# Low part of a split weight behind its high part in one chunk of a query projection (encoder block in fp32 on Trainium2)

## The chip, the cores and the metric

The kernel runs on one core of one Trainium2 chip. The metric is the device time of one execution in microseconds (us). For the kernel before, three runs gave 1444.93, 1439.76 and 1440.73 us; their median is 1440.73 us.

## The reference, cut to what matters

One encoder layer on a sequence of 1024 tokens of width 1024, with 16 learned meta tokens ahead of them, all in float32. Two attention branches read the same projection: branch A is differential attention (4 heads), branch B is windowed grouped-query attention (8 query heads, 2 key and value heads, a window of 128 tokens, and sinks).

```python
h = jnp.concatenate([meta, x], axis=1)
for layer in range(DEPTH):
    h = h + mixer_block(rms_norm(h, norm_mix[layer]), ...)
    h = h + swiglu(rms_norm(h, norm_ffn[layer]), w_ff_gate[layer], w_ff_up[layer], w_ff_down[layer])
return rms_norm(h, norm_final)[:, N_META:]
...
proj = h @ w_in                  # 1024 x 4352: qa, ka, va, qb, kb, vb, ga, gb
y_a = differential_attention(qa, ka, va, ...)
y_b = windowed_gqa(qb, kb, vb, sink)
merged = jax.nn.sigmoid(ga) * (y_a @ w_ba) + jax.nn.sigmoid(gb) * (y_b @ w_bb)
return merged @ w_o
```

The change concerns the part `qb` of `proj`: the queries of branch B. Their 512 columns are worked on in four blocks of 128; the change touches the second block.

## The kernel before, in words

**Products.** Every float32 product is made of three faster products of type fp32r. An operand is split into a high part (a copy that is rounded to fp32r, made by ScalarE, L117) and a low part (the operand less its high part, made by VectorE or GpSimd, L118), and high x high, high x low and low x high are added up in one PSUM bank. A weight column block of 1024 x 128 is loaded by `prep` (L174 to L188): one DMA of 512 KB on SyncE's queue (L180), the high part, then the low part. The low part is GpSimd's work, but for a list of blocks (`on_vector`) and the second query block it is VectorE's.

**A projection** (`project_steps`, L207 to L218) goes over chunks of tokens. One chunk has a PSUM bank (tag "pp", three of them) and 8 steps, one for each 128 rows of the weight (`DC` is 8); a step issues three products (L214): wh with hT_hi, wh with hT_lo, wl with hT_hi. hT_hi and hT_lo are the two parts of the normalised input, transposed. Behind the last step the chunk is evicted (`evac_split`, L227): ScalarE writes the high part, VectorE the low part of a staging tile (qk_stage, three of them), and small DMAs on SyncE's queue move it on: 8 for a chunk of keys (L282, with 8 more at L285 for the last chunk), 4 for a chunk of queries of branch B (L305).

**The start of the program** (L411 to L465) interleaves two things. The normalisation and transposition of nine token tiles (`norm_x`, `turn_x`) make the input, 128 tokens at a time, and three projections use it as it comes in chunks of 256 tokens (`early`): p_kb (keys of branch B), p_q0 and p_q1 (first and second query block). The weights of p_q1 are prepared at L434 under the name qbx; both parts of them stand in one tile, wb_qbx, and the low part is VectorE's work, which also works for the normalisation. So the first chunk of p_q1 (tile pp_qb_0) comes about when its weight has just arrived.

**What follows.** The attention of branch B works in units of 128 tokens (`attend_b`): scores (bps, L331), exps on ScalarE (bs, L337, and a small one, bes, L339), scaling by GpSimd (L343), then, in the unit's second half, transposes (bpt, L356) and value products (bpy, L362). Units 0 and 1 are begun at L502; the others (`units_b`, L655) are worked on together with the projections of branch A (`project_a`, L658 and L660), the first of which is the query block C_QA: its weight is w_c_1019 in the order below, with the parts wh_c_1021 and wl_c_1022, and its products are pp_qa.

**What sets the order.** The code at these places is not the order of the instructions. When the program is built, a scheduler simulates it and decides for each engine what comes next (`SCHED`, L68); by hand stands the order of GpSimd from L691 and of TensorE from L910, and more further down. So a change to one loop can move instructions of other parts, on every engine, up to there. Each engine works its own list off in order, SyncE's list of DMA issues included.

Of the kernel before, what the change touches and what calls it, by code (L numbers as in the profile page):

```python
# [19 lines left out]
P = 128  # L20
# [4 lines left out]
DC = D // P  # L25
# [44 lines left out]
C_QA, C_KA, C_VA, C_QB, C_KB, C_VB, C_GA, C_GB = 0, 512, 1024, 1536, 2048, 2176, 2304, 3328  # L70
# [3 lines left out]
def encoder_block(ctx: ExitStack, tc: tile.TileContext, x, meta, norm_mix, w_in, lq1, lk1, lq2, lk2,  # L74
                  subln, sink, w_ba, w_bb, w_o, norm_ffn, w_g, w_u, w_d, norm_final, out, dbg=None):
    nc = tc.nc
# [5 lines left out]
    def f32(ap):  # L82
        return ap.bitcast(F32)
# [76 lines left out]
    def pp_bank(name):  # L160
        return bank(psum1, "pp", name, 3 if psum1 is not psum2 else PP2)
# [4 lines left out]
    Q_CHUNKS = [(0, 512), (512, 512)]  # L166
    A_CHUNKS = [(0, 392), (392, 392), (784, 256)]
    KB_CHUNKS = [(0, 256), (256, 256), (512, 256), (768, 272)]
    QB_CHUNKS = [(0, 256), (256, 256), (512, 256), (768, 256)]
# [34 lines left out]

    turning_v = []

    def project_steps(col, chunks, name, evac):  # L207
        wh, wl = prepped.pop(col)
        terms = [(wh, hT_hi), (wh, hT_lo), (wl, hT_hi)]
        for at, n in chunks:  # L210
            ps = pp_bank(f"pp_{name}_{at}")
            for c in range(DC):
                for i, (a, b) in enumerate(terms):
                    nc.tensor.matmul(ps[:, :n], a[:, c, :], b[:, c, at:at + n],  # L214
                                     start=(c == 0 and i == 0), stop=(c == DC - 1 and i == 2))
                if c == DC - 1:
                    evac(ps[:, :n], at, n)
                yield  # L218

    def project(col, chunks, name, evac):  # L220
        ensure(1)
        for i, _ in enumerate(project_steps(col, chunks, name, evac)):
            if i % DC == V_AT and turning_v:
                next(turning_v[0], None)
        ensure(W_BUFS - 1)

    def evac_split(scale, consume):  # L227
        def run(ps, at, n):
            st = stage.tile([P, 2, 512], F32R, tag="qk", name="qk_stage", bufs=QK_BUFS)
            hi, lo = st[:, 0, :n], st[:, 1, :n]  # L230
            if scale is None:
                nc.scalar.activation(hi, ps, AF.Copy)
                nc.vector.tensor_tensor(lo, ps, f32(hi), ALU.subtract)
            else:
                nc.scalar.activation(hi, ps, AF.Copy, scale=scale)
                nc.vector.scalar_tensor_tensor(lo, ps, scale, f32(hi), ALU.mult, ALU.subtract)
            consume(f32(st), at, n)
        return run
# [57 lines left out]
    def new_qb(g):  # L296
        return bpool.tile([P, 4, S], F32R, tag="qb", name=f"qb{g}", bufs=1)

    def qb_steps(g, qb, jj):
        j = 2 * g + jj  # L300

        def consume(st, at, n):
            for par in range(2):
                for hl in range(2):
                    nc.sync.dma_start(f32(qb)[64 * hl:64 * hl + 64, 2 * jj + par, at:at + n],  # L305
                                      st[64 * par:64 * par + 64, hl, :n])
        return project_steps(C_QB + j * P, QB_CHUNKS if j < 2 else Q_CHUNKS, f"qb{j}", evac_split(qbs[:, j:j + 1], consume))

    def project_qb(g, qb):
        for jj in range(2):  # L310
            ensure(1)
            for _ in qb_steps(g, qb, jj):
                pass
            ensure(W_BUFS - 1)
# [56 lines left out]
    qb = new_qb(0)  # L371
    qbs = acon.tile([P, 4], F32, name="qbs")
# [56 lines left out]
    norm_x(2)  # L429
    turn_x(1)  # L430
    p_kb = project_steps(C_KB, KB_CHUNKS, "kb", evac_split(None, kb_consume))
    p_q0 = qb_steps(0, qb, 0)
    p_q1 = qb_steps(0, qb, 1)
    prepped[C_QB + P] = prep(C_QB + P, "qbx", lowpool, nc.vector)  # L434
    early += [(p_kb, DC), (p_q0, DC), (p_q1, DC)]
# [257 lines left out]
    qb = new_qb(1)  # L693
# [29 lines left out]
    for k in range(0, 6, 2):  # L723
        ensure(1)
        wh, wl = prepped.pop((k, k + 1))
        for i in range(2):
            ps = pp_bank(f"pg2_{k + i}")
# [265 lines left out]
    def ps_bank(name):  # L993
        return bank(psum3, "bank", name, 8)
# [46 lines left out]
    def gated(i, o, half, w, src):  # L1041
        tk = slice(half * 512, half * 512 + 512)
        gt = ypool.tile([P, 512], F32, tag="gt", name=f"gt_{i}_{o}_{half}", bufs=GT_BUFS)
        nc.sync.dma_start(gt, g_d[8 * i + o][:, tk])
        nc.scalar.activation(gt, gt, AF.Sigmoid)
        ps = ps_bank(f"ppa_{o}_{half}_{i}")
        branch_mm(ps, w, src, tk)
        return gt, ps, tk
# [3 lines left out]
    for o in range(DC):  # L1052
        w = first_w[o] if o < 2 else branch_w(ypool, o, w_bb, "b")
        for half in range(2):
            gt, ps, tk = gated(0, o, half, w, yb)
# [16 lines left out]
    for n, (o, half) in enumerate(order_a):  # L1072
        if o not in ws_a:
            ws_a[o] = branch_w(ypool, o, w_ba, "a")
        gt, ps, tk = gated(1, o, half, ws_a[o], ya)
# [214 lines left out]
    for t in range(4, NT):  # L1290
        ps = ps_bank(f"po_1_{t}")
# [226 lines left out]
    for n in range(nf, len(steps)):  # L1518
        p, j = steps[n][1]
# [3 lines left out]
        if p in LOADS:  # L1523
            at, half, col = LOADS[p]
# [62 lines left out]
```

## Time and profile before

| | before |
|---|---|
| three runs | 1444.93, 1439.76, 1440.73 us (median 1440.73) |
| the profiled execution | 1441.88 us |
| its span in the trace | 1440.0 us |
| mean granted clock of TensorE | 0.998 |
| TensorE matmuls | 1420.1 us busy, 7279 instructions |
| VectorE, ScalarE, GpSimd | 899.8, 680.1, 643.6 us busy |

The profile is one execution as the hardware profiler recorded it. Its span runs from the first instruction to the last; the execution's own time is 1.9 us longer. In the lines below, PE is TensorE, PEld its weight loads, DVE VectorE, ACT ScalarE, POOL GpSimd; SPq is the queue of DMA issues of SyncE. "L214" is the line of the kernel, "pp_qb<-hT_hi,wb_qbx" the output and the inputs by the program's names. In a timeline row the first number is the start and the second the length in us; the time in brackets is how long the engine stood idle just before, and what ended it. In the list of waits the numbers behind a row are the sum, the count and the longest.

### The profile page before, as it was taken

The numbers are of one execution on the slowest core, as the hardware profiler recorded it, in microseconds if no ns is written. First come the engines' busy times: TensorE is split into PE (matmuls) and PEld (weight loads), VectorE is DVE, ScalarE is ACT, GpSimd is POOL, SyncE is SP. The second block draws the span as 40 slices with busy tenths as digits, with TensorE's granted clock in tenths as the row PEclk, the third lists the DMA queues.
The fourth block names the chain that finished last, engine by engine and source line by source line (L and its number), as shares of the span: only waits on it lengthen the run. The fifth ranks groups of instructions, "written<-read, shape, count | busy, mean of one in ns | idle before, by whom it ended". The sixth has DMA issues, their size and how long they took to land.

```text
span 1440.0 us, 21175 instructions
## 1 busy us (share of the span) xinstructions
PE 1420.1 (99%) x7279; PEld 1219.3 (85%) x7279; DVE 899.8 (62%) x1624; ACT 680.1 (47%) x1294; POOL 643.6 (45%) x605
## 2 busy tenths in 40 slices
PE   8999999999999999999999999999999999999997
PEld 6988989988888989888888888888888888888886
DVE  7468536637787978624614886555555554787567
ACT  6366535545565656544413743333333333444444
POOL 5599127744433333334622665554454442000444
PEclk9999999999999999999999999999999999999999
DMA  8367668986657464576612535333323333964443
GB/s 246 87 211 235 194 160 275 282 284 221 181 178 257 145 224 141 175 251 207 210 49 88 162 93 176 99 106 105 110 97 101 104 103 102 340 201 142 124 129 139
DMA packets 188891, 242.41 MB, mean 168 GB/s; under 512 B 18208, under 2 KB 115936, under 8 KB 188784
## 3 DMA queue, kind: packets, MB, share of 16 engines
q1 hardware_dynamic: 188784, 241.07, 53.0%
q8 instruction: 57, 0.93, 0.3%
q14 instruction: 50, 0.41, 0.1%
HBM read 157.45 MB, written 77.00 MB: 163 GB/s over the span
## 4 chain that ended last, share of the span: by engine, by line
PE 86%; issue 3%; DMA 3%; POOL 3%; DVE 2%; ACT 2%; SPq 0%; POOLq 0%; ACTq 0%; DVEq 0%
PE pg L1347 28%; PE pd L1462 9%; PE pg L751 7%; PE ppa L796 6%; PE po L1105 6%; PE aps L814 4%; PE pp_ka L214 3%; PE pp_va L214 3%; PE pp_qa L214 3%; PE pp_qb L214 3%; PE apy L862 3%; POOL oa L118 3%; PE apt L849 2%; PE bpt L356 2%; PE bpy L362 2%
## 5 line engine op out<-in xcount | busy, mean ns | idle before, releaser
L118 POOL TENSOR_TENSOR wop<-wf,wop 128x512 fp32r<-128x512 f32 x128 | 172.0, 1348 | 165.5 <-ACT wop L117 153.1
L1347 PE MATMUL pg<-t,wop 128*128 128x512 f32 x1056 | 242.6, 389 | 0.0
L1347 PEld LDWEIGHTS pg<-t,wop 128*128 128x128 f32 x1056 | 198.3, 188 | 41.1
L1462 PE MATMUL pd<-ob,oa 128*128 128x512 f32 x924 | 210.0, 390 | 0.4 <-POOL oa L118 0.4
L1462 PEld LDWEIGHTS pd<-ob,oa 128*128 128x128 f32 x924 | 173.4, 188 | 36.9 <-POOL oa L118 0.8
L1347 PE MATMUL pg<-b,wop 128*128 128x512 f32 x792 | 183.5, 390 | 1.4 <-DVE kept L1272 1.4
L1347 PEld LDWEIGHTS pg<-b,wop 128*128 128x128 f32 x792 | 148.5, 188 | 32.3 <-issue 1.6
L751 PE MATMUL pg<-hT_hi,gop 128*128 128x512 f32 x384 | 142.4, 395 | 0.0
L117 ACT ACTIVATE wop<-wf 128x512 fp32r<-128x512 f32 x128 | 80.3, 632 | 86.9 <-PE pg L1347 47.7
L118 POOL TENSOR_TENSOR oa<-ra,oa 128x512 fp32r<-128x512 f32 x33 | 44.0, 1335 | 170.2 <-ACT oa L117 168.8
L118 POOL TENSOR_TENSOR gop<-gr,gop 128x512 fp32r<-128x512 f32 x47 | 65.5, 1395 | 102.8 <-ACT gop L117 101.7
L117 ACT ACTIVATE oa<-ra 128x512 fp32r<-128x512 f32 x77 | 48.7, 632 | 107.1 <-PE pd L1462 45.8
L824 ACT ACTIVATE as<-as,amn 128x1040 f32<-128x1040 f32 x64 | 74.5, 1164 | 48.6 <-DVE amn L817 37.7
L814 PE MATMUL aps<-ak,aq 128*128 128x392 f32 (+1 forms) x384 | 89.5, 328 | 2.7 <-DVE amn L817 2.1
L1163 DVE TENSOR_TENSOR s<-wf,wf 128x512 f32<-128x512 f32 x22 | 27.3, 1242 | 101.4 <-DMA wf<-in_w_ff_gate_dram 53.2
L1105 PE MATMUL po<-woh,mT 128*128 128x512 f32 x384 | 88.0, 390 | 0.0
L1105 PEld LDWEIGHTS po<-woh,mT 128*128 128x128 f32 x384 | 71.9, 188 | 14.8
L814 PEld LDWEIGHTS aps<-ak,aq 128*128 128x128 f32 x384 | 69.3, 188 | 16.2 <-DVE amn L817 3.3
L751 PEld LDWEIGHTS pg<-hT_hi,gop 128*128 128x128 f32 x384 | 72.3, 188 | 11.2 <-DVE gk L756 0.2
L343 POOL TENSOR_SCALAR bs<-bs,bdn 128x432 f32<-128x432 f32 (+1 forms) x64 | 41.4, 665 | 87.2 <-DVE bdn L341 74.5
L751 PE MATMUL pg<-hT_lo,gop 128*128 128x512 f32 x192 | 75.9, 395 | 0.0
L828 POOL TENSOR_SCALAR as<-as,adn,neglam 128x1040 f32<-128x1040 f32 x32 | 38.9, 1214 | 62.0 <-DVE adn L826 42.6
(292 smaller groups left out, 3101.7 us busy)
## 6 DMA issues: line engine op xcount, KB each, us to landing
ra<-aop SPq DMA_DIRECT2D x77, 256.0 KB, 2.6
wf<-in_w_ff_gate_dram SPq DMA_DIRECT2D x24, 512.0 KB, 3.8
wf<-in_w_ff_up_dram SPq DMA_DIRECT2D x24, 512.0 KB, 3.8
aop<-as SPq DMA_DIRECT2D x44, 256.0 KB, 2.1
w_c<-in_w_in_dram SPq DMA_DIRECT2D x17, 512.0 KB, 6.1
aop<-c SPq DMA_DIRECT2D x33, 256.0 KB, 2.0
ts_d<-to SPq DMA_DIRECT2D x16, 512.0 KB, 3.7
gw<-in_w_in_dram SPq DMA_DIRECT2D x32, 256.0 KB, 4.3
```

The lines of the kernel that those rows point to most:

```text
L117: nc.scalar.activation(hi, src, AF.Copy)
L118: lo_eng.tensor_tensor(lo, src, f32(hi), ALU.subtract)
L214: nc.tensor.matmul(ps[:, :n], a[:, c, :], b[:, c, at:at + n], start=(c == 0 and i == 0), stop=(c == DC - 1 and i == 2))
L343: nc.gpsimd.tensor_scalar(st[:, r, :W], st[:, r, :W], dn[:, r:r + 1], 1.0, ALU.mult, ALU.mult)
L751: nc.tensor.matmul(ps, op[:, a, c], quad(b, *act)[:, c], start=(p in (2, 5, 1) and c == 0 and i == 0), stop=(p in (2, 3, 4) and c == 3 and ...
L796: nc.tensor.matmul(ps, w[:, a, j, :], src(j, b, tk), start=(j == 0 and n == 0), stop=(j == 3 and n == 2))
L814: nc.tensor.matmul(ps[:, :n], qs[m][:, t * P:(t + 1) * P], ks[m][:, vv, k0:k0 + n], start=(vv == 0), stop=(vv == 1))
L824: nc.scalar.activation(s[m][:, 0:L], s[m][:, 0:L], AF.Exp, bias=low, scale=-1.0, accum_out=dn[:, m:m + 1])
L862: nc.tensor.matmul(py[:, cols], v[:kp, a, k, :], at_[:kp, k, b, :], start=(k == 0 and j == 0), stop=(k == 8))
L1105: nc.tensor.matmul(ps, mT[:, c, a, t * P:(t + 1) * P], wos[q, c][:, b], start=(c == 0 and n == 0), stop=(c == DC - 1 and n == 2))
L1347: nc.tensor.matmul(ps, op[:, x, c, :], b[:, y, c, :], start=(p in (1, 2, 5) and c == 0 and n == 0), stop=(p in (4, 2, 3) and c == 3 and n ...
L1462: nc.tensor.matmul(ps[u], oa[:, a, u * P:(u + 1) * P], ob[:, b, :], start=(p in (1, 2, 5) and j == 0 and k == 0), stop=(p in (2, 3, 4) and ...
```

## The change

In the first chunk (tokens 0 to 255) of the second query block, the products with the weight's low part are taken out of their places. Steps 0 to 6 issue two products each, wh with hT_hi and wh with hT_lo; step 7 issues its two and then the eight products wl with hT_hi. The other chunks of this block and all other projections issue their products as before. The start flag is still on the first product and the stop flag on the last.

```diff
--- before.py
+++ after.py
@@ -204,15 +204,19 @@
 
     turning_v = []
 
-    def project_steps(col, chunks, name, evac):
+    def project_steps(col, chunks, name, evac, low_last=False):
         wh, wl = prepped.pop(col)
         terms = [(wh, hT_hi), (wh, hT_lo), (wl, hT_hi)]
+        each = [[(c, i) for i in range(3)] for c in range(DC)]
+        behind = [[(c, i) for i in range(2)] for c in range(DC)]
+        behind[-1] += [(c, 2) for c in range(DC)]
         for at, n in chunks:
             ps = pp_bank(f"pp_{name}_{at}")
             for c in range(DC):
-                for i, (a, b) in enumerate(terms):
-                    nc.tensor.matmul(ps[:, :n], a[:, c, :], b[:, c, at:at + n],
-                                     start=(c == 0 and i == 0), stop=(c == DC - 1 and i == 2))
+                for k, i in (behind if low_last and at == 0 else each)[c]:
+                    a, b = terms[i]
+                    nc.tensor.matmul(ps[:, :n], a[:, k, :], b[:, k, at:at + n],
+                                     start=(k == 0 and i == 0), stop=(k == DC - 1 and i == 2))
                 if c == DC - 1:
                     evac(ps[:, :n], at, n)
                 yield
@@ -304,7 +308,7 @@
                 for hl in range(2):
                     nc.sync.dma_start(f32(qb)[64 * hl:64 * hl + 64, 2 * jj + par, at:at + n],
                                       st[64 * par:64 * par + 64, hl, :n])
-        return project_steps(C_QB + j * P, QB_CHUNKS if j < 2 else Q_CHUNKS, f"qb{j}", evac_split(qbs[:, j:j + 1], consume))
+        return project_steps(C_QB + j * P, QB_CHUNKS if j < 2 else Q_CHUNKS, f"qb{j}", evac_split(qbs[:, j:j + 1], consume), j == 1)
 
     def project_qb(g, qb):
         for jj in range(2):
```

The scheduler makes another order of the whole first part from it. Beyond about 180 us the order of TensorE is the same. Three places follow; line numbers of the order after are three or four higher, since the function has grown.

The first is TensorE's list at the chunk itself. pp_qb_0_487 is the bank of this chunk, wb_qbx is its weight (both parts have this name), ptn_a_1_339 is a transposition of token tile 4, pp_kb_519 belongs to the second chunk of the keys. Before, the list has:

```order
L214 MATMUL pp_qb_0_487<-hT_hi,wb_qbx 128x256
L214 MATMUL pp_qb_0_487<-hT_lo,wb_qbx 128x256
L148 MATMUL ptn_a_1_339<-ident,xn_a_299 128x128 x4
L214 MATMUL pp_kb_519<-hT_hi,wh_c_192 128x256
L214 MATMUL pp_qb_0_487<-hT_hi,wb_qbx 128x256 x2
L214 MATMUL pp_qb_0_487<-hT_lo,wb_qbx 128x256
L214 MATMUL pp_qb_0_487<-hT_hi,wb_qbx 128x256 x2
L214 MATMUL pp_qb_0_487<-hT_lo,wb_qbx 128x256
L214 MATMUL pp_qb_0_487<-hT_hi,wb_qbx 128x256 x2
```

After, it has:

```order
L218 MATMUL pp_qb_0_487<-hT_hi,wb_qbx 128x256
L218 MATMUL pp_qb_0_487<-hT_lo,wb_qbx 128x256
L218 MATMUL pp_qb_0_487<-hT_hi,wb_qbx 128x256
L148 MATMUL ptn_a_1_339<-ident,xn_a_299 128x128 x4
L218 MATMUL pp_qb_0_487<-hT_lo,wb_qbx 128x256
L218 MATMUL pp_kb_519<-hT_hi,wh_c_192 128x256
L218 MATMUL pp_qb_0_487<-hT_hi,wb_qbx 128x256 x8
L218 MATMUL pp_qb_256_555<-hT_hi,wh_c_237 128x256
```

Before, the first row is the chunk's first product, and each pair "x2" is a product with the low part (the third of its step) and the first of the next step; so the third product of the chunk already takes the low part. After, the rows are the end of the chunk: all sixteen products with the high part stand ahead, the last of them around the transposes, and the eight with the low part are the row "x8", right ahead of the next chunk.

The second place is the list of DMA issues of SyncE, in the same stretch and behind it. kb_146 and kb_147 are the keys of branch B, qb_156 its queries, w_c_1019 is the weight of C_QA, ts_d_91 and ts_d_93 are tables that are written to memory for a later stage (`token_sums`), w_c_1705 is the next weight. Before:

```order
L282 DMA kb_146<-qk_stage 64x2x128 x4
L282 DMA kb_147<-qk_stage 64x2x128 x4
L305 DMA qb_156<-qk_stage 64x256 x6
L180 DMA w_c_1019<-in_w_in_dram 128x8x128
L305 DMA qb_156<-qk_stage 64x256 x2
L282 DMA kb_146<-qk_stage 64x2x128 x2
```

After:

```order
L289 DMA kb_147<-qk_stage 64x8x16
L309 DMA qb_156<-qk_stage 64x256 x8
L180 DMA w_c_1019<-in_w_in_dram 128x8x128
L526 DMA ts_d_91<-to_0_1588 256x1x512
L526 DMA ts_d_93<-to_0_1597 256x1x512
L180 DMA w_c_1705<-in_w_in_dram 128x8x128
```

The load of w_c_1019 stood behind the first 14 of the small DMAs of the chunks (8 for keys, 6 for queries); now it stands behind all 72, right ahead of the first ts_d.

The third place is TensorE's list where the projections of branch A begin. bps_1_1 to bps_2_0 are scores of units 1 and 2, bpy_0 value products and bpt transposes of units 0 and 1. Before, with a pair of scores ahead of it, the list has:

```order
L331 MATMUL bps_1_1_909<-kb_146,qb_156 128x432 x2
L331 MATMUL bps_1_2_913<-kb_146,qb_156 128x432 x2
L331 MATMUL bps_1_3_917<-kb_146,qb_156 128x432 x2
L331 MATMUL bps_2_0_1091<-kb_146,qb_156 128x432 x2
L214 MATMUL pp_qa_0_1645<-hT_hi,wh_c_1021 128x512
L214 MATMUL pp_qa_0_1645<-hT_lo,wh_c_1021 128x512
L214 MATMUL pp_qa_0_1645<-hT_hi,wl_c_1022 128x512
```

After:

```order
L218 MATMUL pp_qa_0_1645<-hT_hi,wh_c_1021 128x512
L218 MATMUL pp_qa_0_1645<-hT_lo,wh_c_1021 128x512
L218 MATMUL pp_qa_512_1675<-hT_hi,wh_c_1021 128x512
L218 MATMUL pp_qa_512_1675<-hT_lo,wh_c_1021 128x512
L366 MATMUL bpy_0_1053<-btr_0_0_1059,vb_148 128x512 x2
L366 MATMUL bpy_0_1053<-btr_0_1_1069,vb_148 128x512
L360 MATMUL bpt_0_8_1074<-ident,bmd_150 128x128 x4
L335 MATMUL bps_2_2_1099<-kb_146,qb_156 128x432 x2
L335 MATMUL bps_2_3_1103<-kb_146,qb_156 128x432 x2
L366 MATMUL bpy_0_1053<-btr_0_1_1069,vb_148 128x512
L360 MATMUL bpt_1_0_1121<-ident,bs_1_901 128x128 x4
L218 MATMUL pp_qa_0_1645<-hT_hi,wl_c_1022 128x512
```

The first pp_qa now stands behind the eight transposes bpt_0_0 and bpt_0_1 of unit 0 and the scores bps_2_1 as well (not shown), which stood behind it before. Between its products with the high part and the first one with the low part wl_c_1022 stand products and transposes of the attention units.

GpSimd's list at that stretch (tal and ta are sums of `token_sums`, bmd a small copy) is before:

```order
L118 TENSOR_TENSOR wl_c_938<-w_c_935,wh_c_937 128x1024
L118 TENSOR_TENSOR wl_c_1022<-w_c_1019,wh_c_1021 128x1024
L343 TENSOR_SCALAR bs_0_868<-bs_0_868,bdn_0_870 128x288 x4
L347 COPY bmd_150<-bs_0_868 128x4x32
L526 TENSOR_TENSOR tal_1_1615<-hT_lo 128x512
L343 TENSOR_SCALAR bs_1_901<-bs_1_901,bdn_1_903 128x432 x4
```

and after:

```order
L118 TENSOR_TENSOR wl_c_938<-w_c_935,wh_c_937 128x1024
L543 TENSOR_TENSOR ta_0_1607<-ta_0_1607,hT_lo 128x512
L347 TENSOR_SCALAR bs_0_868<-bs_0_868,bdn_0_870 128x288 x4
L347 TENSOR_SCALAR bs_1_901<-bs_1_901,bdn_1_903 128x432
L351 COPY bmd_150<-bs_0_868 128x4x32
L347 TENSOR_SCALAR bs_1_901<-bs_1_901,bdn_1_903 128x432 x3
L118 TENSOR_TENSOR wl_c_1022<-w_c_1019,wh_c_1021 128x1024
```

The low part of C_QA's weight, wl_c_1022, came ahead of the scaling of units 0 and 1 and now comes behind both. On ScalarE its high part, wh_c_1021, stood right behind the evictions of the last query chunk; now it stands behind the exps of unit 1 and bes_1.

## Prediction before the run

> **What bounds the kernel now.** The page comes first: how much of the span TensorE (PE) is busy.
>
> ```profile
> span 1440.0 us, 21175 instructions
> PE 1420.1 (99%) x7279; PEld 1219.3 (85%) x7279; DVE 899.8 (62%) x1624; ACT 680.1 (47%) x1294; POOL 643.6 (45%) x605
> ```
>
> PE is idle for 1440.0 - 1420.1 = 19.9 us in all, so a change that adds and removes no product can win little, and it loses whatever new idle time it makes on PE. The second view is the list of PE's waits, cut to 20 to 180 us, since beyond 180 us the built order of PE is the same before and after.
>
> ```profile
> PE pp_qb L214 <- DVE wb_qbx L118: 1.5, 1, 1.5
> PE bps L331 <- DVE bmn L333: 1.0, 3, 0.5
> ```
>
> The first row is the wait the change aims at. The third view is PE's timeline around it, and VectorE's row that ends it.
>
> ```profile
> 21.62 0.36 PE L214 MATMUL pp_qb<-hT_hi,wb_qbx 128*128 128x256 f32 x1
> 21.82 0.28 PE L214 MATMUL pp_qb<-hT_lo,wb_qbx 128*128 128x256 f32 x1
> 21.94 0.60 PE L148 MATMUL ptn_a<-ident,xn_a 128*128 128x128 f32 x4
> 22.30 0.36 PE L214 MATMUL pp_kb<-hT_hi,wh_c 128*128 128x256 f32 x1
> 24.18 0.50 PE L214 MATMUL pp_qb<-hT_hi,wb_qbx 128*128 128x256 f32 x2 [1.51 <-DVE wb_qbx L118]
> ...
> 26.41 0.40 PE L214 MATMUL pp_qb<-hT_hi,wb_qbx 128*128 128x256 f32 x2
> 26.65 0.28 PE L214 MATMUL pp_qb<-hT_lo,wb_qbx 128*128 128x256 f32 x1
> 26.77 0.28 PE L214 MATMUL pp_qb<-hT_hi,wb_qbx 128*128 128x256 f32 x1
> ```
>
> ```profile
> 22.91 1.22 DVE L118 TENSOR_TENSOR wb_qbx<-w_qbx,wb_qbx 128x1024 fp32r<-128x1024 f32 x1
> ```
>
> PE runs two products of the chunk, then sits for 1.51 us until the low part (22.91 + 1.22 = 24.13) is there.
>
> **The change part by part.**
>
> *The chunk itself.* The same 24 products run, 14 more of them ahead of the first that needs the low part. From 26.41 to 26.77 three products pass, 0.12 us each, so 14 take 1.65 us. They start where PE now starts to wait (22.66) and end at 24.3, when the low part is 0.15 us old. The whole wait of 1.51 us goes, and nothing takes its place here: -1.5 us. Between 24.18 and 69 us the list has no other wait of PE, so this lead lasts to about 67 us.
>
> *What the built order moves besides.* The fourth view is SyncE's queue, because the order puts the load of w_c_1019 (weights of the first query projection, C_QA) behind 58 other DMA issues.
>
> ```profile
> 20.74 5.93 SPq L282 DMA_DIRECT2D kb<-qk_stage  x8
> 26.77 3.74 SPq L305 DMA_DIRECT2D qb<-qk_stage  x6
> 30.56 0.59 SPq L180 DMA_DIRECT2D w_c<-in_w_in_dram  x1
> ...
> 66.00 5.91 SPq L305 DMA_DIRECT2D qb<-qk_stage  x8
> 71.96 1.26 SPq L522 DMA_DIRECT2D ts_d<-to  x2
> 73.31 2.29 SPq L180 DMA_DIRECT2D w_c<-in_w_in_dram  x2
> ```
>
> SyncE issues without a pause worth the name from 20.74 to 71.9 us, about 0.7 us for each small DMA (5.91 / 8), though VectorE has evicted the last of these chunks long before. The queue is its own limit, so PE's lead does not shorten it; only the load taken out of its middle does (30.56 to 31.24, 0.7 us). The load is thus issued at 71.9 - 0.7 = 71.2 us in place of 30.56. How long it takes then, the next three rows bound: the answer for L180 in a window around 30.56 us, one around 96 us, and one around 73.3 us, where it stands behind two 512 KB writes.
>
> ```profile
> DMA to landing us min/median/max: 4.8/4.8/4.8
> DMA to landing us min/median/max: 4.3/4.3/4.3
> DMA to landing us min/median/max: 6.5/6.8/7.2
> ```
>
> Ends 4.3 and 6.5 us; I take 4.8, since both loads that had no other large transfer ahead lie near it and in the new order the load is ahead of the writes. It lands at 76.0. ScalarE has its exps of unit 1 behind it by then (the 75.76 row below, earlier with the lead), and makes the high part in 1.06 us:
>
> ```profile
> 75.76 0.19 ACT L339 ACTIVATE bes<-bes 128x4 f32<-128x4 f32 x1
> 79.88 1.06 ACT L117 ACTIVATE wh_c<-w_c 128x1024 fp32r<-128x1024 f32 x1 [1.75 <-DMA w_c<-in_w_in_dram]
> ```
>
> The second row shows the same kind of wait already: the next weight, loaded at 73.31, holds up ScalarE until 79.8, and nobody behind it. So the first product of C_QA can start at 76.0 + 1.06 + 0.1 = 77.2 us. Now PE's rows at that place:
>
> ```profile
> 72.80 0.67 PE L331 MATMUL bps<-kb,qb 128*128 128x432 f32 x2 [0.46 <-DVE bmn L333]
> 73.31 0.40 PE L214 MATMUL pp_qa<-hT_hi,wh_c 128*128 128x512 f32 x1
> 73.55 0.40 PE L214 MATMUL pp_qa<-hT_lo,wh_c 128*128 128x512 f32 x1
> ...
> 78.21 0.82 PE L356 MATMUL bpt<-ident,bs 128*128 128x128 f32 x6
> ...
> 85.57 0.63 PE L362 MATMUL bpy<-btr,vb 128*128 128x512 f32 x2
> ```
>
> Now C_QA starts at 73.31, with all that stands ahead of it done. After the change it starts at 77.2, +3.9. What PE does sooner counts against that: the eight transposes of unit 0 (78.21 row: six in 0.6 start to start, so 0.8) and one pair of scores (0.4 to 0.5) have moved ahead of it, 1.2 us. Net +2.7 us at this point; the 1.5 us won earlier are spent in it, since the load sets the start whether PE is early or not.
>
> *The low part of the same weight.* GpSimd makes it, and its order puts it behind the scaling of units 0 and 1:
>
> ```profile
> 53.80 4.75 POOL L118 TENSOR_TENSOR wl_c<-w_c,wh_c 128x1024 fp32r<-128x1024 f32 x2
> 73.35 1.96 POOL L343 TENSOR_SCALAR bs<-bs,bdn 128x288 f32<-128x288 f32 x4 [14.80 <-DVE bdn L341]
> 77.95 2.86 POOL L343 TENSOR_SCALAR bs<-bs,bdn 128x432 f32<-128x432 f32 x4
> ```
>
> Unit 0 is scaled by about 74.5 (the 73.35 row, less 0.8 of lead), unit 1 needs 2.86 and the small copy 0.3 more: 77.7. Then 4.75 / 2 = 2.4 for the low part: 80.1 us. PE meanwhile has four products of 512 columns (0.93), four value products (0.93, same width), eight transposes (0.8) and two pairs of scores (0.8): 77.2 + 3.5 = 80.7. It waits little for GpSimd, but its value products hang on VectorE's evictions; I add 0.2. By the same list of work before stood at 73.31 + 1.2 + 3.5 = 78.0. So PE is 80.9 - 78.0 = 2.9 us late, and from here it is busy all the time, as it was:
>
> ```profile
> 80.00:100.00 20.00, 20.00 (x110) 18.20 (x108) 14.52 (x30) 12.65 (x28) 19.41 (x18) 1.00 0.72 218
> 100.00:120.00 20.00, 20.00 (x132) 19.26 (x131) 16.00 (x31) 13.69 (x32) 19.00 (x17) 1.00 0.50 169
> 120.00:140.00 20.00, 19.97 (x111) 17.17 (x110) 16.12 (x31) 12.21 (x29) 19.92 (x20) 1.00 0.87 247
> ```
>
> The columns are the window, its length, then PE, PEld, DVE, ACT and POOL busy, the clock and DMA. PE has no idle time there in which 2.9 us could be made good, and behind 180 us its order is unchanged: the loss stays to the end. The other moved steps I cost at nothing: the attention units of the first group run earlier against the projections, the products are the same. GpSimd is the cover (19 to 19.9 of 20 us busy): adding its durations up in the new order, the scaling of units 2 to 7 is ready at least 2.8 us ahead of the transposes that need it. If that cover is gone, each us of it is a us of PE.
>
> **Sum.** -1.5 won, then +4.4 in the new wait (77.2 against 73.31 with 1.2 less left to do, and the lead spent), together +2.9 us. The profiled execution took 1441.88 us, 1.9 more than its span: 1441.88 + 2.9 = 1444.8. It lies 1.15 above the median of the three runs; from 1440.73 the same sum is 1443.6. I forecast 1444. With a landing in 4.3 us it would be 0.5 less; in 6.5 us, 1.7 more: own range 1442.5 to 1446.5.
>
> **Rivals.**
>
> *The load comes in time.* If SyncE's issues go out as fast as their data are ready, the last of them leave near 58 us (VectorE evicts the last chunk at 57.25), the load lands by 63, PE at 72 us finds its weights, and only the gain is left: 1441.88 - 1.6 = 1440.3, from the median 1439.1; say 1439.7. Against it stand the six SyncE rows, in which an issue costs 0.7 us each time. It decides if the queue ends before about 66 us. The Trainium skill, "DMA: Bandwidth & Descriptors", section "Issuing engines are not separate DMA queues", says that the sequencer's time to start a DMA is usually small beside the DMA; by that rule this rival would hold, and the trace speaks against it, 0.7 us a piece. Chance 0.13.
>
> *The clock falls.* PE is done with unit 0 at about 74.8 and idles to 77.2, 2.4 us, behind a stretch that is half empty. The end of the program shows a fall of the clock after an idle time:
>
> ```profile
> 1426.30 6.64 PE L1462 MATMUL pd<-ob,oa 128*128 128x512 f32 x28 [0.42 <-POOL oa L118]
> 1435.00:1440.00 5.00, 0.00 (x0) 0.00 (x0) 0.75 (x1) 0.82 (x2) 0.48 (x1) 0.56 0.56 210
> ```
>
> The last product ends at 1432.94, and a mean clock of 0.56 over 1435 to 1440 means 1 for 0.6 us and 0.5 for the rest: it falls 2.7 us after. If 2.4 us or a longer landing trips it, about 4 us of products run at half speed, half of that lost: 1444 + 2 = 1446. The Trainium skill, "TensorE: Matmul & The Clock Gate", section "What's actually happening", puts the fall after one idle window of about 3.4 us, free-running; the trace's 2.7 fits inside it, and by the page 2.4 us would mostly be survived. Chance 0.10.
>
> *GpSimd becomes the bound* (slower by over 0.5%). The low part of C_QA (2.4 us) was made in its idle time (the 14.80 us ahead of 73.35) and now stands in its full stretch. If the 2.8 us of cover is not there, PE waits for the scaling of units 2 and 3, 2.86 us each: 1444 + 5.7 = 1449.7. Against it: the cover counted above, and before not one wait of PE for GpSimd in this stretch. Chance 0.07.
>
> The change does do what it says, since the order shows it.
>
> **How the numbers follow.** Forecast 0.70, at 1444; the rivals 0.13, 0.10 and 0.07. The range 1440.0 to 1447.5 holds the forecast with both landings, the clock's fall and half of the first rival; left out are GpSimd (0.07), the other half (0.06) and an edge of the rest. About 0.5%, 7.2 us, is what a measurement here tells from no change: only the third rival, 0.07, and 0.01 of accidents lie above it; nothing named lies below 1433.5, I leave 0.01 for it. Within: 0.91. Slower than before by any amount has 0.85.
>
> **What would show it.** Right: no wait of PE for wb_qbx near 22.7 us; SyncE busy to about 71 us and the C_QA load issued there; a wait of PE of 2 to 3 us at the first pp_qa for ScalarE's wh_c, which starts when the load lands, near 76 us; the first pp_qa low-part product near 81 us; the same lag of about 3 us at 180 us. Wrong: pp_qa starting near 73 us; a clock below 1 in the 75 to 85 us slices; waits of PE for GpSimd between 85 and 150 us; or a lag that melts before 180 us, which would mean that PE's order had slack that I don't see.

## The result, and the profile after

The changed kernel takes 1444.53 us in the median of 20 executions (1441.69 to 1451.07) against 1441.53 us before (20 executions, 1439.76 to 1444.93): ratio 1.0022, 95% interval 1.0015 to 1.0029. It is 3.0 us slower, within the 0.5% that the prediction calls no change.

One trap first. The profiled execution of the changed kernel is the fastest of its 20 (1441.69 us), and its span, 1439.9 us, is that of before. Its TensorE was 1.2 us late at 17 us, since the clock fell there (granted 0.83 from 10 to 20 us, before 1.00), and it was 2.2 us behind before at 200 us; between 330 and 410 us it had caught up, because the profiled execution of before lost 2 us more there than it did, in waits that differ from one execution to the next. A single profile can hide 3 us of 1440. So the changed kernel was profiled twice more, in executions of 1445.98 us (the second) and 1445.54 us (the third), and the lines below are of the second where nothing else is said.

PE's waits between 20 and 180 us, first of the first profile, then of the second:

```profile
PE bps L335 <- DVE bmn L337: 1.5, 3, 0.8
PE pp_qa L218 <- ACT wh_c L117: 0.6, 1, 0.6
```

```profile
PE bps L335 <- DVE bmn L337: 1.5, 3, 0.8
PE pp_qa L218 <- ACT wh_c L117: 1.5, 1, 1.5
```

The wait for wb_qbx is gone from both, and a wait for the high part of C_QA's weight has come. PE's timeline of the second profile at the chunk: the last products with the high part, a key product, and the eight with the low part in a row.

```profile
23.75 0.37 PE L218 MATMUL pp_qb<-hT_lo,wb_qbx 128*128 128x256 f32 x1
23.95 0.28 PE L218 MATMUL pp_kb<-hT_hi,wh_c 128*128 128x256 f32 x1
24.08 1.21 PE L218 MATMUL pp_qb<-hT_hi,wb_qbx 128*128 128x256 f32 x8
```

Nothing is idle there. To say how far PE is ahead or behind, each product and transpose is weighed with its usual distance to the next (0.118 us at 256 columns, 0.227 at 512, 0.109 for a transpose), and the times at which the same sum of work is reached are compared with the first profile of before. By that, the second profile is 1.8 us ahead at 30 us. The late load then takes it all back. SyncE's queue, the landing of the load (the answer for L180 in a window around 71 us) and ScalarE's row:

```profile
65.75 5.05 SPq L309 DMA_DIRECT2D qb<-qk_stage  x8
70.84 0.59 SPq L180 DMA_DIRECT2D w_c<-in_w_in_dram  x1
71.48 1.28 SPq L526 DMA_DIRECT2D ts_d<-to  x2
```

```profile
DMA to landing us min/median/max: 4.5/4.5/4.5
```

```profile
75.34 1.06 ACT L117 ACTIVATE wh_c<-w_c 128x1024 fp32r<-128x1024 f32 x1 [1.59 <-DMA w_c<-in_w_in_dram]
```

And PE there:

```profile
73.71 1.22 PE L360 MATMUL bpt<-ident,bs 128*128 128x128 f32 x6
76.45 0.50 PE L218 MATMUL pp_qa<-hT_hi,wh_c 128*128 128x512 f32 x1 [1.52 <-ACT wh_c L117]
...
77.41 0.63 PE L218 MATMUL pp_qa<-hT_lo,wh_c 128*128 128x512 f32 x1
77.84 1.48 PE L366 MATMUL bpy<-btr,vb 128*128 128x512 f32 x3
...
81.58 0.47 PE L218 MATMUL pp_qa<-hT_hi,wl_c 128*128 128x512 f32 x1
```

The reader sees two things. The load is issued at 70.84 us, so C_QA starts at 76.45 in place of 73.31 us. And behind the wait the products are slower: from 77.41 to 77.84 one product of 512 columns takes 0.43 us from start to start, where it took 0.23 before. That is the granted clock. Busy times by stretch, in the columns of the prediction (PE second, clock last but two), of before and then of the first, second and third profile of the changed kernel:

```profile
70.00:77.00 7.00, 6.00 (x26) 4.16 (x25) 5.25 (x20) 5.01 (x18) 2.58 (x6) 1.00 0.66 195
77.00:81.00 4.00, 4.00 (x23) 3.39 (x23) 2.23 (x5) 1.76 (x3) 4.00 (x6) 1.00 1.08 331
```

```profile
70.00:77.00 7.00, 5.01 (x22) 2.86 (x22) 4.43 (x20) 6.03 (x19) 3.72 (x8) 1.00 0.78 244
77.00:81.00 4.00, 3.94 (x22) 2.95 (x21) 4.00 (x8) 3.54 (x9) 3.47 (x4) 1.00 0.53 155
```

```profile
70.00:77.00 7.00, 4.30 (x18) 2.53 (x19) 3.48 (x16) 5.09 (x17) 4.52 (x9) 1.00 0.78 241
77.00:81.00 4.00, 4.00 (x15) 3.34 (x14) 4.00 (x9) 3.00 (x7) 3.37 (x4) 0.57 0.51 156
```

```profile
70.00:77.00 7.00, 4.93 (x18) 3.02 (x16) 3.94 (x18) 4.79 (x17) 3.97 (x9) 0.76 0.72 215
77.00:81.00 4.00, 3.72 (x12) 2.95 (x13) 3.25 (x8) 2.66 (x6) 3.31 (x5) 0.57 0.70 217
```

Before, PE is idle for 1.0 of the 7 us; after, for 2.0 to 2.7. In two of the three executions the clock fell in this stretch: for 0.43 x 4 / 0.5 = 3.4 us in the second, and for 0.24 x 7 / 0.5 more, together 6.8 us, in the third. In the second the fall begins at 77.0 us, behind the wait for the weight. In the third it begins at 73.6 us (77 less 3.4), ahead of that wait, which lasts from 76.3 to 77.3 us: what lies ahead of this fall are waits of the scores for bmn, 1.2 of the 3.4 us from 70.2 us on. So the wait for the load isn't the only thing that makes the clock fall here; the denser mix of scores ahead of it can do it too.

At 92 us the three are 2.3, 3.5 and 4.2 us behind before, and at 200 us 2.2, 3.4 and 4.1 us. How far such a figure can be trusted, a second profile of the kernel before tells (an execution of 1442.97 us; ten executions, median 1442.59 us, ratio 1.0009, 0.9995 to 1.0022, expected 1.000): its clock is 1.00 from 70 to 90 us, as was expected if the change makes the falls, and it is 0.2 us behind the first at 92 us, but 1.4 us at 200 us, in waits for VectorE's evictions that the first has not. So up to 92 us the two profiles of before agree, and the lags stand out; behind it, executions of the same kernel differ by more than 1 us. The late load and the order that goes with it cost about 2 us net of the lead even when the clock stays, and 1 to 2 us more when it falls.

### The profile page after: what moved, and what is told of

Read it like the earlier page. It is cut to its first block, busy times and chain, and to the rows that moved or that the text cites. A ratio compares the mean times of both kernels' runs of the same rounds, so it can differ in the third digit from the quotient of the medians.

```text
span 1439.9 us, 21171 instructions
## 1 busy us (share of the span) xinstructions
PE 1422.3 (99%) x7279; PEld 1220.9 (85%) x7279; DVE 908.0 (63%) x1624; ACT 679.4 (47%) x1294; POOL 643.5 (45%) x605
## 4 chain that ended last, share of the span: by engine, by line
PE 86%; POOL 4%; issue 4%; DMA 3%; DVE 2%; ACT 1%; SPq 0%; POOLq 0%; DVEq 0%; ACTq 0%
PE pg L1351 28%; PE pd L1466 9%; PE pg L755 7%; PE ppa L800 6%; PE po L1109 6%; PE aps L818 3%; PE pp_ka L218 3%; PE pp_va L218 3%; PE pp_qb L218 3%; PE pp_qa L218 3%; PE apy L866 3%; POOL oa L118 3%; PE apt L853 2%; PE bpt L360 2%; PE bpy L366 2%
```

## The experiments

Every ratio is against the kernel before, run between the others on the same chip.

**Early load.** The changed kernel; the load of C_QA's weight is built with a higher priority (... stands for code left out, here and below).

```diff
+            if col == C_QA:
+                with tc.high_priority():
+                    nc.sync.dma_start(w, w_in[:, col:col + P].rearrange("(c p) n -> p c n", p=P))
...
```

> The changed kernel, and in it the load of the weight of C_QA with a higher priority in the built order: it stands behind 6 of the 72 small DMAs in SyncE's list again, not behind all of them. Theory 1 (the late load is the whole loss): the first chunk runs without its wait and the first pp_qa finds its weight, so TensorE is about 1.8 us ahead of before from 27 us on and keeps it past 90 us: 1441.5 - 1.8 = 1439.7 us, ratio 0.9988. Theory 2 (the new interleaving of scores, transposes and products costs it, whatever the load does): about 1444, ratio 1.002.

Measured: 1442.19 us, ratio 1.0001 (0.9991 to 1.0010). The loss is gone, so the load, with the order that goes with it, is what cost it; but nothing is won either, and theory 1 wanted 0.9988. The order has changed too: C_QA starts at 70.67 us, in the midst of the scores, so that the wait for the load and the denser mix of scores ahead of it are gone together. Its profile shows the load in time and where the lead of 1.8 us goes. SyncE's row, PE's waits, ScalarE at the first of these, and PE at the last:

```profile
25.32 0.55 SPq L182 DMA_DIRECT2D w_c<-in_w_in_dram  x1
```

```profile
PE bps L339 <- DVE bmn L341: 2.1, 3, 1.4
PE pp_vb L222 <- DVE qk_stage L244: 0.8, 1, 0.8
```

```profile
52.47 0.40 ACT L240 ACTIVATE qk_stage<-pp_kb 128x272 fp32r<-128x272 f32 x1 [2.49 <-DMA qb<-qk_stage]
...
57.26 0.48 ACT L243 ACTIVATE qk_stage<-pp_qb,qbs 128x256 fp32r<-128x256 f32 x1 [2.05 <-DMA qb<-qk_stage]
```

```profile
88.34 0.65 PE L339 MATMUL bps<-kb,qb 128*128 128x432 f32 x2 [1.39 <-DVE bmn L341]
```

Near 55 us pp_vb waits 0.8 us for the eviction of a query chunk, and ScalarE's evictions wait for DMAs out of the staging tiles. These are the small DMAs of SyncE's queue: PE cannot run ahead of it by more than three staging tiles. The lead falls from 1.6 us at 51 us to 0.55 at 61. It is 1.4 us again at 75 us, since the first profile of before waits for bmn there and this one hardly does; 1.6 us go near 88 us, in a wait for VectorE, in the new mix of scores and projections, and 1.4 us more between 102 and 115 us, where the second profile of before loses 0.7 us as well. Theory 1 holds for the loss and fails for the gain.

**Late load.** The kernel before, with its chunk unchanged; the load stands behind all 72 small DMAs. For that the order of SyncE over this stretch is by hand, and the weight of the value projection of branch B (C_VB) is prepared ahead of it.

```diff
...
+    order.remove(C_VB)
+    prepped[C_VB] = prep(C_VB, f"c{C_VB}")
+    with tc.manual_schedule(engines={mybir.EngineType.SP}):
+        advance(100)
+        ahead[C_QA] = wpool.tile([P, DC, P], F32, tag="w", name=f"w_c{C_QA}", bufs=2)
+        nc.sync.dma_start(ahead[C_QA], w_in[:, C_QA:C_QA + P].rearrange("(c p) n -> p c n", p=P))
```

> The kernel before with its chunk unchanged, and in it only the load of the weight of C_QA put behind all 72 small DMAs of the chunks (the order of SyncE over that stretch is by hand). Theory 1: the wait of 1.5 us at the chunk is still there, and the load lands near 75 to 76 us as after the change, so the first pp_qa starts near 76.5 us, by about 2.7 us too late; TensorE being early or late at the chunk makes no difference, since the load sets the time: 1444.3 us, ratio 1.002, the same as the changed kernel. Theory 2: the load alone costs nothing, about 1441.5, ratio 1.000. If lead and wait simply add up (theory 3), it is slower than the changed kernel by the 1.5 us of the lead: 1446, ratio 1.003.

Measured: 1449.33 us, ratio 1.0046 (1.0030 to 1.0063), from six executions: worse than any of the theories had it. The load is issued at 71.33 us and C_QA starts at 76.74, as expected. But the scheduler also put two products of the next weight (pp_va) ahead of C_QA's low part, which makes a second wait for a load, and the clock falls twice (waits, then busy times by stretch):

```profile
PE pp_qb L218 <- DVE wb_qbx L118: 1.8, 1, 1.8
PE pp_va L218 <- ACT wh_c L117: 1.5, 1, 1.5
```

```profile
75.00:78.00 3.00, 2.89 (x10) 1.94 (x10) 0.54 (x2) 1.28 (x4) 3.00 (x7) 0.52 1.01 353
78.00:81.00 3.00, 2.19 (x8) 1.09 (x7) 2.34 (x4) 2.30 (x4) 3.00 (x3) 0.91 0.61 192
...
84.00:87.00 3.00, 3.00 (x8) 2.31 (x7) 0.00 (x0) 0.54 (x2) 3.00 (x2) 0.50 0.98 270
```

PE is 9 us behind at 92 us. The first of the two falls begins at 75.1 us, ahead of C_QA, behind waits for bmn like that of the third profile. That a late load slows the kernel without the change at the chunk is shown; by how much isn't, since the order changed in a second place.

**The changed kernel again.**

> The changed kernel itself once more, for a second profiled execution. The first one was the fastest of 20 (1441.69 us against a median of 1444.53) and began 1.2 us late. Theory 1: about 1444.5 us, ratio 1.002; a profile of a usual execution has TensorE waiting at the first pp_qa for 1.5 to 2.5 us, since it comes there earlier and the load does not, and it is 2 to 3 us behind before at 200 us. Theory 2: the wait at the first pp_qa stays at 0.6 us and the rest is lost elsewhere.

> The changed kernel once more, on the same chip and in the same rounds as the filled one, so that the two can be set against each other. Ratio 1.002; the third profile shows whether the clock falls between 77 and 81 us in this execution (it did in one of two); the mean granted clock over all executions is about 0.001 below that of the kernel before.

Measured: 1444.33 us, ratio 1.0018 (1.0006 to 1.0030), and 1443.59 us, ratio 1.0010 (1.0001 to 1.0020). Their profiles are shown above. The wait at pp_qa is 1.5 and 1.0 us. The mean granted clock over all 43 executions of the changed kernel is 0.99772, over 93 of the kernel before 0.99861: 0.0009 x 1444 = 1.3 us of full clock lost, about half of the difference of the means (1444.4 against 1442.0 us). A mean clock of 0.997 or less stands in 16 of the 43 and in 5 of the 93. Both figures count falls at any place, the one near the start of the first profile too.

**The wait filled, first try.** The changed kernel; the two blocks of unit 0 are each transposed three times.

```diff
-                for r in range(4):
+                for r in range(12 if (g, t) == (0, 0) and k < 8 else 4):
+                    r %= 4
```

> The changed kernel, with 16 transposes more: the two blocks of scores of unit 0 of branch B are each transposed three times into the same bank, not once, in the place where TensorE waits for the weight of C_QA. The order is that of the changed kernel at this place. The load is as late as before, so the start of the first pp_qa stays near 76.4 us: the added 1.75 us of work lies in the wait. Theory C (the fall of the granted clock that the second profile of the changed kernel shows from 77 to 81 us, 0.57, follows from the idle time ahead of it and is a good part of the loss): the clock stays 1.00 there, and the time falls by some 1 us (1.6 us where the clock had fallen, nothing where it had not): 1443.3, ratio 1.0013. Theory D (the clock plays no part in the median): 1444.4 or a little more, ratio 1.002.

Measured: 1445.47 us, ratio 1.0019 (1.0009 to 1.0029). It tells nothing for or against the clock, since the idle time only moved: the evictions of these blocks now stand behind the added transposes, and the value products wait for them. The clock then falls one step later (waits, and the stretch from 81 to 85 us):

```profile
PE bpy L367 <- DVE btr L365: 1.6, 1, 1.6
...
PE bpy L367 <- ACT btr L363: 0.9, 1, 0.9
```

```profile
81.00:85.00 4.00, 3.19 (x10) 2.81 (x11) 3.56 (x9) 2.63 (x5) 2.37 (x3) 0.61 0.65 190
```

**The wait filled elsewhere.** The changed kernel; the added transposes go to the bank of the value products, which is written anew behind them.

```diff
...
+            if (g, t) == (0, 0):
+                ready = {b[0]: turned(*b) for b in blocks[:2]}
+                for r in range(16):
+                    nc.tensor.transpose(py[:, r % 4 * P:r % 4 * P + P], st[:, r % 4, 0:P], ident)
...
```

> The changed kernel with 16 transposes more in the place where TensorE waits for the weight of C_QA, this time into a bank that nobody reads before it is written anew, so that no eviction stands behind them (in the first try the tripled blocks held up the evictions, and the wait moved to bpy). Nothing of the output is touched. Theory C (the granted clock falls because TensorE stands idle ahead of the first pp_qa, and this is about half of the median loss of 3 us): the clock stays 1.00 from 77 to 85 us in the profile, the first pp_qa still starts near 76.4 us, and the median is about 1 to 1.5 us below that of the changed kernel: 1443.2, ratio 1.001. Theory D (the clock plays no part): as the changed kernel, 1444.4, ratio 1.002, or more.

The same with `range(10)`:

> The changed kernel with 10 transposes more in the wait ahead of the first pp_qa, into the same bank as before (16 of them made pp_qa start at 77.05 us, 0.7 us behind the 76.3 to 76.5 us at which the weight was there in the two profiles of the changed kernel). Theory C: pp_qa starts near 76.4 us again, the clock stays 1.00 to 85 us, and the ratio is 1.000 to 1.001, below that of the changed kernel in the same comparison. Theory D (the clock plays no part, or falls whether the wait is filled or not): the same ratio as the changed kernel, 1.002.

Measured: with 16, 1441.98 us, ratio 1.0008 (1.0000 to 1.0017); with 10, 1442.06 us, ratio 0.9998 (0.9987 to 1.0008), beside 1.0010 for the changed kernel in the same comparison. PE and its clock with 16, then with 10 (13 and 7 of the added transposes stand in the first row, three in each case among the transposes ahead of it):

```profile
75.37 1.58 PE L367 MATMUL bpy<-ident,bs 128*128 128x128 f32 x13
77.05 0.50 PE L218 MATMUL pp_qa<-hT_hi,wh_c 128*128 128x512 f32 x1
```

```profile
77.00:81.00 4.00, 3.95 (x22) 3.32 (x23) 3.49 (x8) 3.08 (x7) 3.37 (x5) 1.00 0.68 203
```

```profile
75.23 0.93 PE L367 MATMUL bpy<-ident,bs 128*128 128x128 f32 x7
76.92 0.50 PE L218 MATMUL pp_qa<-hT_hi,wh_c 128*128 128x512 f32 x1 [0.77 <-ACT wh_c L117]
```

```profile
77.00:81.00 4.00, 4.00 (x22) 3.20 (x23) 3.61 (x8) 3.02 (x7) 3.37 (x4) 1.00 0.66 203
```

More work, and over all executions a shorter time: 1442.5 us in the mean (23, both filled) against 1444.4 us (43). Against the kernel before in their own comparisons the filled kernels are 0.8 and 0.2 us slower in the mean, the changed kernel 2.9, 2.8 and 1.7 us. PE is not sooner at the first pp_qa, and the clock stays at 1.00 in both profiles, as theory C has it. Both profiles are of long executions (1445.97 and 1445.24 us); they are 2.7 and 2.5 us behind before at 92 us, near the 2.3 us of the changed kernel where its clock stayed.

That the gain is the clock's is not shown, though. The clock stayed in one of three profiles without the filling as well, and in the third it fell ahead of the place that is filled. The mean granted clock of the filled kernels is 0.99830, which makes up 0.8 of the 2.0 us between the means. In the only comparison that has both kernels the intervals overlap, and the clocks are 0.99827 and 0.99818, worth 0.1 us, where the means differ by 1.5 us. Theory C may hold for a part; where the rest comes from is open. The filled kernel is a probe, not a cure: the load is still late.

**Two queues.** The changed kernel, and the kernel before, with the 16 query DMAs of the tokens from 512 on issued from ScalarE.

```diff
-                    nc.sync.dma_start(f32(qb)[64 * hl:64 * hl + 64, 2 * jj + par, at:at + n],
+                    (nc.scalar if j < 2 and at >= 512 else nc.sync).dma_start(f32(qb)[64 * hl:64 * hl + 64, 2 * jj + par, at:at + n],
```

> The changed kernel with the 16 small query DMAs of the last two pairs of chunks (tokens from 512 on) issued from ScalarE's queue in place of SyncE's. Theory 1' (SyncE's queue is the bound of this stretch: it holds up both the load and, through the staging tiles, the evictions that the lead of 1.8 us needs): SyncE is through with the chunks some 10 us earlier, the load comes in time, TensorE has no wait at pp_vb near 54 us, and the lead is kept: 1.8 us faster than the kernel before with the same edit, about 1439.7 us. Rival: ScalarE, which now has 16 issues of about 0.6 us each among its evictions, holds TensorE up instead: 1442 to 1446 us, and no difference to the kernel before with the same edit.

> The changed kernel with the 16 late query DMAs on ScalarE's queue once more, since the first comparison rested on five executions. Theory 1' (SyncE's queue was what ate the lead): ratio 0.997 to 0.9985. If the first result was luck: 1.000.

> The kernel before with the same edit as in the other run: the 16 small query DMAs of the last two pairs of chunks go out from ScalarE's queue. The wait of 1.5 us at the chunk stays, and nothing else in it waits for SyncE's queue: 1441.5 us, ratio 1.000; under the rival, with ScalarE holding TensorE up, 1442 to 1446.

Measured: the changed kernel with two queues 1437.48 us, ratio 0.9968 (0.9956 to 0.9981, five executions), and again 1438.80 us, ratio 0.9984 (0.9975 to 0.9992, eleven); the kernel before with two queues 1442.91 us, ratio 1.0002 (0.9993 to 1.0011). This is the only version here that is faster than the kernel before, by 2.3 to 4.6 us. SyncE's load and PE's stretches in the second execution of it:

```profile
49.99 0.60 SPq L180 DMA_DIRECT2D w_c<-in_w_in_dram  x1
```

```profile
40.00:60.00 20.00, 20.00 (x154) 20.00 (x154) 7.71 (x15) 6.38 (x13) 15.61 (x10) 1.00 0.61 157
...
70.00:77.00 7.00, 7.00 (x32) 5.83 (x32) 4.14 (x13) 3.70 (x12) 4.24 (x7) 1.00 0.88 251
```

The load goes out at 50 us, PE has no wait at pp_vb and none at pp_qa, and it is 1.7 to 2.0 us ahead of before from 40 us to 320 us, but for some us near 70 where the order of the scores differs: the lead of the chunk, kept. The pair doesn't isolate the chunk, though. With two queues the kernel before got another wait, for a write of the tables, and a fall of the clock behind it (waits, then 75 to 77 us). In this one profile it is 3.2 us behind before at 200 us; the median of the eleven executions shows no loss, and how often the fall comes isn't known.

```profile
PE pv_vb L252 <- DMA ts_d<-to: 1.7, 1, 1.7
```

```profile
75.00:77.00 2.00, 2.00 (x6) 1.52 (x6) 1.11 (x6) 1.76 (x5) 0.71 (x2) 0.50 1.13 301
```

## Why the prediction was right, point by point

- *The chunk.* The wait goes and hardly anything takes its place there: right. From 20 to 30 us it was worth 1.8, 1.7 and 1.2 us in the three profiles (1.5 forecast); in the third the low part came only at 24.9 us, so that some 0.3 us of the wait was left. (The 1.51 us are counted from the end of the product at 22.66; from start to start, 22.30 to 24.18 us, the place cost 1.88 us where 0.12 is usual.)
- *"This lead lasts to about 67 us."* Wrong in part. The list of waits of before has nothing between 24 and 69 us because PE was late enough. With PE ahead, the staging tiles became a wait near 55 us: 0.8 us with the early load, 0.9 and 0.6 in two of the filled kernels, 0.4 in the second profile, hardly any in the first and third, which led by 0.5 and 0.9 us only. The forecast didn't need the lead, since the load sets the start of C_QA.
- *SyncE's queue is its own limit, and the load goes out at 71.2 us.* Right: 71.0, 70.8 and 71.4 us. It landed in 4.1, 4.5 and 4.8 us (4.8 taken).
- *C_QA starts at 77.2 us.* It was 76.3, 76.5 and 77.3.
- *A wait of 2 to 3 us at the first pp_qa.* Too long: it was 0.6, 1.5 and 1.0 us. The prediction's own figures for it don't agree: its sum has 4.4 us, with the lead spent in the wait, but this sign and the rival of the clock have PE there at 74.8 us, without the lead. PE came at 75.7, 74.9 and 76.3 us, since part of the lead had gone, or had never come, and the scores ahead wait 1.5 us for bmn in place of 1.0. The moved steps, which the prediction costs at nothing, cost these 0.5 us.
- *The low part near 81 us.* Without the fall of the clock the first such product stood at 80.29 us (80.9 forecast), with it at 81.6 and 82.3.
- *GpSimd's cover holds.* Right: no profile of the changed kernel shows PE waiting for GpSimd between 85 and 180 us.
- *The lag stays.* Right: 2.3, 3.5 and 4.2 us at 92 us and 2.2, 3.4 and 4.1 us at 200 us, against 2.9.
- *The clock.* The term that failed. The prediction had the fall as a rival with a chance of 0.10 that needs the one long wait at pp_qa; it took part in two of three executions, with single waits of 1.5 us at most, and in the third it came ahead of that wait. By the mean granted clock it costs 1.3 us. The rival's 2.7 us from the last product to the fall at the end of the program are no fixed delay either: in the other profiles of both kernels they are 2.2 (the third) to 5.3 us (the second). The plain wait was mis-sized the other way: 2.2 us at 200 us where the clock stayed, not 2.9. That these errors work against each other, so that the total, 1444, is this near to 1444.5, is luck.
- *The chances.* By the prediction's own list the range holds 0.70 + 0.10 + 0.065 = 0.865, not 0.91.

The size of the whole is thus right, in part by luck, and a good half of it for the reason that was forecast. What stays open: how much of the 2.2 us without a fall is the load itself and how much the denser mix of scores and transposes ahead of it (the waits for bmn went from 1.0 to 1.5 us). The early load removes both together. Open too is how much of the loss is the clock's: its mean says about half, but the filled kernels, which win back 2.0 us, have only 0.8 us of it in their clock.

## What to carry to other kernels

A product moved off a late operand is worth its wait only as long as nothing behind it, a DMA queue or a ring of staging tiles, runs at its own pace: look at the busiest issue queue before you count a lead as time. Where a scheduler sets the order, look first for the load that has changed places. And price an idle stretch of TensorE by what it does to the clock as well.

## What the runs showed that was not expected

- The clock falls without a long gap. In the second profile the longest idle time was 1.5 us, and PE was busy for 4.3 of the 7 us ahead of the fall; in the third no wait ahead of it was over 0.8 us, and PE was busy for 2.0 of 3.4 us. The falls lasted 3.4 and 6.8 us. The Trainium skill, "TensorE: Matmul & The Clock Gate", section "HAM oscillation — how this bites in real kernels", warns of idle gaps of over some 3.4 us. The traces here fell at less than half of that, so the measurement decides: a stretch that is 60% busy isn't safe. The lengths of the falls agree with the window of about 3.4 us that the page gives. But such a stretch doesn't always make the clock fall: in the kernel before, PE is busy for 1.9 of the 3.4 us from 22.5 us on, around the wait of 1.5 us, and for 2.0 of the 3.4 us from 811 us on, and the clock stays at 1.00. What decides isn't shown.
- Useless transposes in an idle stretch made the kernel faster (1442.5 against 1444.4 us in the means), and the clock shows only a part of why.
- A small DMA costs its queue 0.63 to 0.7 us of issue, on ScalarE's queue as on SyncE's, so 72 of them fill 50 us. With 16 of them moved to ScalarE the changed kernel is 2.3 to 4.6 us faster than before, where it is 3 us slower without. ScalarE's queue in the second execution with two queues, four issues of 0.63 us:

```profile
43.61 2.54 ACTq L309 DMA_DIRECT2D qb<-qk_stage  x4
```

- Tiny VectorE instructions can be long where GpSimd is busy. In the run with the early load a sum of 128 x 4 elements took 1.63 us, where its like takes 0.15 us elsewhere in the same run; it stands ahead of the scores' reduction that PE then waits for near 88 us. In the kernel before one takes 2.3 us, near 131 us, with no wait of PE behind it. The cause wasn't tried.

```profile
L348 DVE TENSOR_TENSOR bdn<-bdn,bes 128x4 f32<-128x4 f32 x1 | 1.6, 1632 | 0.0
```
